# Expert outputs weighted on VectorE out of PSUM, and expert rows gathered one block earlier

## The chip, the cores and the metric

One core of a Trainium2 chip runs the whole program. It has five engines with queues of their own that run in order: TensorE (PE in the profile, its weight loads PEld), VectorE (DVE), ScalarE (ACT), GpSimd (POOL) and SyncE (SP), and 16 DMA engines that all queues share. The metric is the time of one execution in microseconds on the device; lower is better.

## What is computed

Two transformer-like blocks run one after the other on 512 tokens (plus 16 meta tokens in the first) of 1024 features. Only the last stage of the second block is touched, the mixture of experts:

```python
def block(args):                       # one padded group of rows of one expert
    tok, w, e = args
    y = swiglu(h[tok], w_gate[e], w_up[e], w_down[e])
    return y * w[:, None]
ys = lax.map(block, (row_tok..., row_w..., blk_e))
return jax.ops.segment_sum(ys.reshape(n_rows, d), row_tok, num_segments=n_tok)
...
x = x + g2 * moe_ffn(...)              # 64 experts, 6 of them for each token
return rms_norm(x, final_g)
```

Each token goes to 6 of 64 experts. An expert has a gate and an up matrix (1024 x 256 each) and a down matrix (256 x 1024). Its output rows are multiplied by the token's weight for this expert and by the vector `g2`, and added to the token's row. All of it is in fp32.

## The kernel before

Everything ahead of the experts (two mixers, the norm, the router, the shared expert) fills the first 2150 us of the span and is not touched. The router leaves index tables in SBUF: which token stands in which row of which block, and where its weight lies. `hn_d`, `w_d` and `moe_d` are DRAM tensors: the normed rows, the weights of (token, expert), and the sum that the experts add to.

The experts run as 31 units in a fixed `ORDER`. A unit is one expert with one or two blocks of rows: 128 and 128, 128 and 64, 128, 64, or 32. That makes 43 blocks: 24 of 128 rows, 7 of 64, 12 of 32. The first 37 blocks hold all those of 128 and 64 rows and 6 of 32; the last 6 are all of 32 rows. For one block the kernel does this:

- `Block.gather`: an indirect DMA on GpSimd's queue brings the rows of the block from `hn_d` into the tile `xg` (3 buffers).
- `Block.turn`: a second indirect DMA brings the 4-byte weights of the rows into `wg`; then `turned` transposes `xg` on TensorE into PSUM (`small`), and ScalarE and VectorE split it into a high and a low part (`exh`, `exl`).
- `Block.piece`: the next step of `expert`: the gate and up matmuls into PSUM (`proj`), SiLU on ScalarE and the product on VectorE (`ea`), two transposes, a split (`eah`, `eal`), and the down matmuls into the PSUM tile `big`, which the code calls `po`.
- `Block.add`, by `added`: ScalarE copies `po` times the weight into `ey` (2 buffers), GpSimd multiplies `ey` by `g2s`, and an indirect DMA on GpSimd's queue adds the rows of `ey` to `moe_d`. The last two blocks instead use two VectorE instructions that read PSUM and do both products at once. Below, that indirect DMA with the add is called the scatter.

The weights of an expert are three 1 MB tiles (`eraw`, 5 buffers, loaded by SyncE's queue), each split by ScalarE (`swh` or `ewh`) and VectorE (`swl` or `ewl`, 128x2048, the longest VectorE instructions of the stage).

The order on GpSimd's and SyncE's queue is that of the code, since both are under `manual_schedule`; on the other engines the scheduler keeps close to it. The loop runs over the blocks and works on three at a time. In turn `i` it finishes block `i-1`, turns block `i+1`, starts the matmuls of block `i`, gathers rows for block `i+2` and adds block `i-2`. A scatter waits for the one before it to have landed, since both add to `moe_d`. An instruction that writes `ey` waits until the scatter two blocks earlier has read and landed it.

```python
if i + 1 < len(blocks):
    blocks[i + 1].turn()
if b:
    if i:
        b.piece(4)
    if i and i + 2 < len(blocks):
        blocks[i + 2].gather()
...
if i > 1:
    blocks[i - 2].add()
```

Of the kernel before, what the change touches and what calls it, by code (L numbers as in the profile page):

```python
# [11 lines left out]
AF = mybir.ActivationFunctionType  # L12
# [1911 lines left out]

ORDER = [0, 19, 1, 20, 2, 15, 9, 12, 3, 21, 4, 22, 5, 16, 10, 13, 6, 23, 7, 24, 8, 17, 11, 14, 18, 25, 26, 27, 28, 29, 30]
STEPS = (0, 4, 10)
ROWS = SEQ + P


# [12 lines left out]
def moe(k, out):  # L1942
    nc, tc, io = k.nc, k.tc, k.io
    mult, add, sub = ALU.mult, ALU.add, ALU.subtract
    tt = nc.vector.tensor_tensor
    ts = nc.vector.tensor_scalar
    stt = nc.vector.scalar_tensor_tensor
    hn_d = k.dram.tile([ROWS, D], F32, name="hn_d")
    moe_d = k.dram.tile([ROWS, D], F32, name="moe_d")
    w_d = k.dram.tile([(SEQ + 1) * NE, 1], F32, name="w_d")  # L1950
# [6 lines left out]
    g2 = swp.tile([P, D], F32, name="g2s", bufs=1)  # L1957
# [139 lines left out]
    with ExitStack() as ctx:  # L2097
# [12 lines left out]
        def gather(bp, name, src, ix, bufs):  # L2110

            x = bp.tile([ix.shape[0], src.shape[1]], F32, name=name, bufs=bufs)
            nc.gpsimd.indirect_dma_start(out=x[:], out_offset=None, in_=src[:, :],
                                         in_offset=bass.IndirectOffsetOnAxis(ap=ix, axis=0))
            return x
# [26 lines left out]
                k.split(hi[:, j:j + nt], lo[:, j:j + nt], pt[:, :nt * n].rearrange("p (a b) -> p a b", a=nt))  # L2142
            return (lambda kt: (hi[:, kt], lo[:, kt])) if n == P else lambda kt: both[:, kt, :2 * n]

        def added(ix, wg, po, n, bp, last=False):

            y = bp.tile([n, D], F32, name="ey")
            if last:
                for hf in range(2):
                    sl = slice(hf * 512, hf * 512 + 512)  # L2150
                    stt(y[:, sl], po[0][:, hf], wg[:], g2[:n, sl], op0=mult, op1=mult)
            else:
                nc.scalar.activation(y[:].rearrange("p (a b) -> p a b", a=2), po[0], AF.Copy, scale=wg[:])  # L2153
                nc.gpsimd.tensor_tensor(y[:], y[:], g2[:n], op=mult)  # L2154
            nc.gpsimd.indirect_dma_start(out=moe_d[:, :], out_offset=bass.IndirectOffsetOnAxis(ap=ix, axis=0),  # L2155
                                         in_=y[:], in_offset=None, compute_op=add)

        with ExitStack() as c4:
# [55 lines left out]
            with tc.high_priority():  # L2214
# [7 lines left out]
                po = k.small()[:, :256].rearrange("p (a b) -> p a b", a=4)  # L2222
                for t in range(4):
                    for u in range(t + 1):
                        nc.tensor.matmul(po[:, t], lhsT=before if u == t else k.ones[:], rhs=mk[:, u], start=u == 0, stop=u == t)
            step(STEPS[0])

            with tc.high_priority():
# [16 lines left out]
                raws = [raw_of(es[0], i) for i in range(3)]  # L2245
            step(STEPS[1])

# [20 lines left out]
            with tc.high_priority():  # L2268
# [9 lines left out]
                sl = rp.tile([P, 4, TOPK], F32, name="sl")  # L2278
# [60 lines left out]
        ep = c3.enter_context(tc.tile_pool(reuse_waits="tile", name="mo_e", bufs=2))  # L2339
        bp = c3.enter_context(tc.tile_pool(reuse_waits="tile", name="mo_b", bufs=2))  # L2340
        wp = c3.enter_context(tc.tile_pool(reuse_waits="tile", name="mo_w", bufs=3, side="right"))
        class Block:
# [4 lines left out]
                self.ix, self.wx = idx[:self.n, col:col + 1], widx[:self.n, col:col + 1]  # L2347

            def gather(self):
                self.x = gather(bp, "xg", hn_d, self.ix, 3)  # L2350

            def turn(self):
                self.wg = gather(bp, "wg", w_d, self.wx, 4)
                self.po = []
                self.run = expert(turned(self.x, self.n, bp), self.n, self.unit.views, ep, self.po, AF.Silu)

# [2 lines left out]
                    next(self.run, None)  # L2359

            def add(self):
                added(self.ix, self.wg, self.po, self.n, ep, self in blocks[-2:])

        class Unit:
            def __init__(self, u, odd):
# [14 lines left out]
        blocks = [b for u in units for b in u.blocks]  # L2380
        ET = mybir.EngineType
        with tc.manual_schedule(engines={ET.Pool, ET.SP}):
            with tc.manual_schedule(engines={ET.PE, ET.Activation, ET.DVE}):
                blocks[0].gather()
                blocks[1].gather()
                nc.gpsimd.dma_start(w_d[:SEQ * NE].rearrange("(t p e) o -> p t (e o)", t=4, p=P), wd[:])
                blocks[2].gather()
                blocks[0].turn()
                units[0].weights(3 - len(units[0].w))
                units[1].weights(1)  # L2390
                blocks[0].piece(4)
            for i, b in enumerate(blocks + [None]):
                prev, ahead = blocks[i - 1] if i else None, []
                if i:
                    prev.piece()
                if i + 1 < len(blocks):
                    blocks[i + 1].turn()
                if b:
                    if i:
                        b.piece(4)  # L2400
                    if i and i + 2 < len(blocks):
                        blocks[i + 2].gather()
                    u = units.index(b.unit)
                    new = b is blocks[0] or b.unit is not prev.unit
                    if u + 1 < len(units):
                        ahead = [units[u + 1]] * (3 - len(b.unit.blocks))
                if i > 1:
                    blocks[i - 2].add()
                if b and new:
                    b.unit.weights(3 - len(b.unit.w))  # L2410
                if ahead:
                    u = ahead.pop()
                    u.weights(min(1, 3 - len(u.w)))
                if b:
                    b.piece()
                if i:
                    prev.piece(3)
                if ahead:
                    u = ahead.pop()
                    u.weights(min(1, 3 - len(u.w)))  # L2420
            blocks[-1].add()
        n = nc.values_load(nb_i[0:1, 0:1], min_val=0, max_val=(MB - NSTAT) // UNR,  # L2422
                           skip_runtime_bounds_check_because="at most MB columns")
        with tc.For_i(0, n, 1) as i:  # L2424
            ix = bp.tile([P, 2, UNR], I32, name="lix")
            be = bp.tile([1, UNR], I32, name="lbe")
            o = i * UNR + NSTAT
            nc.vector.tensor_copy(ix[:, 0], idx[:, bass.ds(o, UNR)])
            nc.vector.tensor_copy(ix[:, 1], widx[:, bass.ds(o, UNR)])
            nc.vector.tensor_copy(be[:], be_i[0:1, bass.ds(o, UNR)])  # L2430
            for u in range(UNR):
                e = nc.values_load(be[0:1, u:u + 1], engines=(mybir.EngineType.SP,), min_val=0, max_val=NE - 1,
                                   skip_runtime_bounds_check_because="six bits")
                x, wg = gather(bp, "xg", hn_d, ix[:, 0, u:u + 1], 3), gather(bp, "wg", w_d, ix[:, 1, u:u + 1], 4)
                ws, po = views([weights(e, j, u % 2) for j in range(3)]), []
                for _ in expert(turned(x, P, bp), P, ws, ep, po, AF.Silu):
                    pass
                added(ix[:, 0, u:u + 1], wg, po, P, ep)
# [9 lines left out]
        for t in range(4):  # L2448
            m, x = ms[t], fp.tile([P, D], F32, name="fx")
# [139 lines left out]
```

## Time and profile before

| | |
|---|---|
| median of 3 runs | 2648.27 us (2647.36 to 2651.03) |
| profiled execution, its own time | 2661.41 us |
| its span, from first to last instruction | 2659.4 us |
| mean granted TensorE clock | 0.934 |
| PE, DVE, ACT, POOL busy in the span | 87%, 70%, 50%, 41% |
| instructions | 41153 |

The busy shares are means over the whole program, and TensorE leads in them. The expert stage, from 2150 us on, is another picture: there the DMA engines are busy for four fifths of the time and GpSimd for three quarters, against a third each before it. What the change is worth must be read from that stage alone: from its windows, from who waited for whom in it, and from the order of time on GpSimd's queue.

### The profile page before, as it was taken

The page shows a single profiled execution, that of the slowest core. Times are in us where ns is not written, and L with a number is a line of the kernel's source. Part 1 is how long each engine was busy: PE and PEld are TensorE (multiplying, and loading weights), DVE is VectorE, ACT ScalarE, POOL GpSimd, SP SyncE. Part 2 cuts the span into 40 slices and gives each one's busy share as a digit, 9 for nine tenths or more (in the row PEclk, how much of TensorE's full clock was granted, in tenths as well). Part 3 has the DMA queues.
Part 4 walks back from the last instruction along what each step waited for, and adds up shares of the span by engine and source line. Part 5 has one row for each costly group of instructions (what it writes and reads, how often), then busy time and mean ns, then how long its engine had stood idle before and what let it go on. Part 6 is the DMA issues. An engine that isn't in the chain of part 4 may idle for free. (4 is left out here: it accounts for less than half of the span.)

```text
span 2659.4 us, 41153 instructions
## 1 busy us (share of the span) xinstructions
PE 2304.5 (87%) x15509; PEld 2016.5 (76%) x15509; DVE 1851.1 (70%) x3276; ACT 1334.1 (50%) x2302; POOL 1084.4 (41%) x694
## 2 busy tenths in 40 slices
PE   6989999999884899999889888988997988888884
PEld 5889999999874888888887887666777766666652
DVE  7788877878676477778878547766375576655575
ACT  5434433434421477777667535532345346555564
POOL 4234443333020454444444022433120048777786
PEclk9999999999996899999999998999798999988887
DMA  4222222222776422222111532233235178887885
GB/s 142 86 71 86 85 78 70 77 84 80 223 231 205 132 72 68 76 80 80 64 44 45 187 112 78 80 96 115 85 107 181 67 268 278 274 258 252 260 282 170
DMA packets 136367, 354.18 MB, mean 133 GB/s; under 512 B 26042, under 2 KB 51147, under 8 KB 124008
## 3 DMA queue, kind: packets, MB, share of 16 engines
q1 hardware_dynamic: 124120, 314.17, 35.4%
q0 software_dynamic: 10608, 32.14, 5.0%
q10 hardware_dynamic: 1440, 5.24, 0.6%
q8 instruction: 123, 2.02, 0.3%
q14 instruction: 76, 0.62, 0.1%
HBM read 301.54 MB, written 49.94 MB: 132 GB/s over the span
## 5 line engine op out<-in xcount | busy, mean ns | idle before, releaser
L180 POOL TENSOR_TENSOR wl<-wr,wh 128x1024 fp32r<-128x1024 f32 x159 | 409.6, 2578 | 629.1 <-ACT wh L179 523.1
L186 PE MATMUL proj<-yhi,wh 128*128 128x264 f32 (+2 forms) x1800 | 584.1, 325 | 11.8 <-ACT yhi L173 5.0
L187 PE MATMUL proj<-ylo,wh 128*128 128x264 f32 (+2 forms) x1800 | 577.8, 321 | 5.0 <-POOL ylo L180 3.2
L188 PE MATMUL proj<-yhi,wl 128*128 128x264 f32 (+2 forms) x1800 | 576.1, 320 | 0.0
L186 PEld LDWEIGHTS proj<-yhi,wh 128*128 128x128 f32 x1800 | 354.8, 197 | 33.2 <-ACT yhi L173 6.4
L187 PEld LDWEIGHTS proj<-ylo,wh 128*128 128x128 f32 x1800 | 354.5, 197 | 24.4 <-POOL ylo L180 4.1
L188 PEld LDWEIGHTS proj<-yhi,wl 128*128 128x128 f32 x1800 | 354.8, 197 | 20.5 <-issue 2.3
L179 ACT ACTIVATE wh<-wr 128x1024 fp32r<-128x1024 f32 x159 | 168.2, 1059 | 222.8 <-PE proj L187 166.9
L2155 POOL DMA_INDIRECT moe_d<-ey,idx x43 | 118.1, 2746 | 60.8 <-DMA moe_d<-ey,idx 30.6
L174 DVE TENSOR_TENSOR ewl<-eraw,ewh 128x2048 fp32r<-128x2048 f32 x45 | 111.9, 2489 | 32.7 <-ACT ewh L173 32.7
L174 DVE TENSOR_TENSOR swl<-eraw,swh 128x2048 fp32r<-128x2048 f32 x46 | 116.9, 2541 | 25.0 <-ACT swh L173 24.0
L186 PE MATMUL big<-oh,wh 128*128 128x256 f32 (+1 forms) x400 | 116.2, 295 | 17.7 <-ACT oh L173 7.6
L188 PE MATMUL big<-oh,wl 128*128 128x256 f32 (+1 forms) x400 | 115.9, 292 | 4.5 <-DVE wl L174 4.4
L187 PE MATMUL big<-ol,wh 128*128 128x256 f32 (+1 forms) x400 | 116.5, 294 | 0.1
L1176 ACT ACTIVATE ex<-big,mx 128x528 f32<-128x528 f32 x128 | 88.5, 696 | 55.0 <-DVE mx L1172 53.2
L2154 POOL TENSOR_TENSOR ey<-ey,g2s 128x1024 f32<-128x1024 f32 (+2 forms) x41 | 104.3, 2544 | 24.9 <-ACT ey L2153 24.0
L857 DVE SCALAR_TENSOR_TENSOR adw<-adw,ada_c 128x512 f32<-128x512 f32 x96 | 71.5, 756 | 46.5 <-DMA adw<-ada_w 45.8
L1172 DVE TENSOR_REDUCE mx<-big 128x1 f32<-128x528 f32 x128 | 84.9, 697 | 22.9 <-PE big L1171 22.6
L173 ACT ACTIVATE swh<-eraw 128x2048 fp32r<-128x2048 f32 x46 | 87.7, 1908 | 18.0 <-PE proj L188 14.8
L186 PEld LDWEIGHTS big<-oh,wh 128*128 128x128 f32 x400 | 78.1, 197 | 20.9 <-ACT oh L173 9.0
L2141 PE MATMUL small<-ident,xg 128*128 128x128 f32 (+2 forms) x344 | 45.4, 267 | 53.8 <-DMA xg<-hn_d,idx 52.2
L1056 ACT ACTIVATE sw<-proj 32x264 f32<-32x264 f32 (+1 forms) x192 | 86.5, 451 | 4.0 <-DVE qk L1053 1.2
(639 smaller groups left out, 6859.3 us busy)
## 6 DMA issues: line engine op xcount, KB each, us to landing
eraw<-ew SPq DMA_DIRECT2D x93, 1024.0 KB
wr<-hy_w SPq DMA_DIRECT2D x64, 512.0 KB
adw<-ada_w SPq DMA_DIRECT2D x96, 256.0 KB
wr<-mx_w SPq DMA_DIRECT2D x31, 512.0 KB
dm<-dmain SPq DMA_DIRECT2D x16, 512.0 KB
wr<-hy_wo SPq DMA_DIRECT2D x16, 512.0 KB
wr<-da_wz SPq DMA_DIRECT2D x16, 512.0 KB
wr<-da_wk SPq DMA_DIRECT2D x16, 512.0 KB
```

Of the source, the lines that this page charges most:

```text
L173: act = self.nc.scalar.activation(hi, src, AF.Copy)
L174: self.nc.vector.tensor_tensor(lo, src, hi.bitcast(F32), op=ALU.subtract)
L179: act = self.nc.scalar.activation(hi, src, AF.Copy)
L180: self.nc.gpsimd.tensor_tensor(lo, src, hi.bitcast(F32), op=ALU.subtract)
L186: mm(out, lhsT=a[0], rhs=b[0], start=start, stop=False)
L187: mm(out, lhsT=a[0], rhs=b[1], start=False, stop=False)
L188: mm(out, lhsT=a[1], rhs=b[0], start=False, stop=stop)
L1056: nc.scalar.activation(sw[a:a + 32, sl], ps[b:b + 32], AF.Copy, scale=sgn)
L1172: nc.vector.tensor_reduce(mx[:, m:m + 1], ps[:, :, :TH], axis=AX.XY, op=ALU.min)
L1176: nc.scalar.activation(e[:, :T].rearrange("p (a b) -> p a b", a=2), ps[:, :, :TH], AF.Exp, bias=mx[:, m:m + 1], scale=-1.0, accum_out=sm[: ...
L2154: nc.gpsimd.tensor_tensor(y[:], y[:], g2[:n], op=mult)
L2155: nc.gpsimd.indirect_dma_start(out=moe_d[:, :], out_offset=bass.IndirectOffsetOnAxis(ap=ix, axis=0), in_=y[:], in_offset=None, compute_op=add)
```

## The change

`added` loses its ScalarE and GpSimd instructions: every block is now weighted by two VectorE `scalar_tensor_tensor` instructions of 512 columns each, which read `po` in PSUM, the weight as a scalar of each row and `g2`, and write `ey`. The rows are gathered three blocks ahead (`AHEAD`) into 4 buffers instead of 3. The gather of the weights leaves `turn`: it is issued in the turn of the block itself, one turn later than before, and behind the gather of rows.

```diff
+AHEAD = 3
-        def added(ix, wg, po, n, bp, last=False):
+        def added(ix, wg, po, n, bp):
             y = bp.tile([n, D], F32, name="ey")
-            if last:
-                for hf in range(2):
-                    sl = slice(hf * 512, hf * 512 + 512)
-                    stt(y[:, sl], po[0][:, hf], wg[:], g2[:n, sl], op0=mult, op1=mult)
-            else:
-                nc.scalar.activation(y[:].rearrange("p (a b) -> p a b", a=2), po[0], AF.Copy, scale=wg[:])
-                nc.gpsimd.tensor_tensor(y[:], y[:], g2[:n], op=mult)
+            for hf in range(2):
+                sl = slice(hf * 512, hf * 512 + 512)
+                stt(y[:, sl], po[0][:, hf], wg[:], g2[:n, sl], op0=mult, op1=mult)
...
-                self.x = gather(bp, "xg", hn_d, self.ix, 3)
+                self.x = gather(bp, "xg", hn_d, self.ix, AHEAD + 1)
+            def weight(self):
+                self.wg = gather(bp, "wg", w_d, self.wx, 4)
             def turn(self):
-                self.wg = gather(bp, "wg", w_d, self.wx, 4)
...
-                blocks[2].gather()
+                for b in blocks[2:AHEAD]:
+                    b.gather()
...
-                    if i and i + 2 < len(blocks):
-                        blocks[i + 2].gather()
+                    if i + AHEAD < len(blocks):
+                        blocks[i + AHEAD].gather()
+                    b.weight()
```

On GpSimd's queue, from the turn of block 2 on (its gathers of weights and rows, its product and its scatter, for two blocks), there stood before:

```order
L2113 DMA wg<-w_d,widx 128x1
L2113 DMA xg<-hn_d,idx 128x1024
L2154 TENSOR_TENSOR ey<-ey,g2s 128x1024
L2155 DMA moe_d<-ey,idx 640x1024
L2113 DMA wg<-w_d,widx 128x1
L2113 DMA xg<-hn_d,idx 32x1024
L2154 TENSOR_TENSOR ey<-ey,g2s 128x1024
L2155 DMA moe_d<-ey,idx 640x1024
```

And in the changed kernel, from the same turn on, for three blocks:

```order
L2114 DMA xg<-hn_d,idx 32x1024
L2114 DMA wg<-w_d,widx 32x1
L2152 DMA moe_d<-ey,idx 640x1024
L2114 DMA xg<-hn_d,idx 128x1024
L2114 DMA wg<-w_d,widx 128x1
L2152 DMA moe_d<-ey,idx 640x1024
L2114 DMA xg<-hn_d,idx 128x1024
```

Each block now has three instructions there instead of four, the rows come first behind a scatter, and they are those of the block after the one that stood there before (the 32 rows are already gathered ahead of the first scatter).

On VectorE, where the stage's fourth block is turned (`exl`), before:

```order
L174 TENSOR_TENSOR eal<-small,eah 128x256
L174 TENSOR_TENSOR exl<-small,exh 128x512 x2
L174 TENSOR_TENSOR ewl<-eraw,ewh 128x2048
L1997 TENSOR_TENSOR elow<-proj,elow 32x512
L174 TENSOR_TENSOR ewl<-eraw,ewh 128x2048
```

And in the changed kernel:

```order
L174 TENSOR_TENSOR eal<-small,eah 128x256
L2151 SCALAR_TENSOR_TENSOR ey<-big,wg,g2s 128x512
L174 TENSOR_TENSOR exl<-small,exh 128x512
L2151 SCALAR_TENSOR_TENSOR ey<-big,wg,g2s 128x512
L174 TENSOR_TENSOR exl<-small,exh 128x512
L174 TENSOR_TENSOR ewl<-eraw,ewh 128x2048
L1998 TENSOR_TENSOR elow<-proj,elow 32x512
L2151 SCALAR_TENSOR_TENSOR ey<-big,wg,g2s 128x512 x2
L174 TENSOR_TENSOR ewl<-eraw,ewh 128x2048
```

The two products of a block stand between or ahead of the splits that TensorE's next block needs. ScalarE's and TensorE's work is otherwise the same, and SyncE's order does not change.

## Rows read from the trace of the kernel before

**Rows 1.** Windows: ahead of the experts and experts; busy PE, PEld, DVE, ACT, POOL, clock, DMA share, GB/s.

```profile
0.00:2150.00 2150.00, 1891.12 (x13601) 1719.11 (x13602) 1525.07 (x2976) 1042.93 (x1987) 712.75 (x515) 0.94 0.32 105
2150.00:2642.00 492.00, 413.42 (x1910) 297.37 (x1908) 320.93 (x297) 286.56 (x308) 365.51 (x171) 0.91 0.80 253
```

**Rows 2.** The same columns: first scatter to 38th, and from there to the end.

```profile
2190.00:2598.00 408.00, 349.49 (x1598) 255.08 (x1597) 263.80 (x227) 245.65 (x264) 318.20 (x148) 0.92 0.86 269
2598.00:2642.00 44.00, 27.65 (x123) 12.97 (x121) 29.24 (x25) 20.05 (x22) 31.90 (x13) 0.87 0.40 119
```

**Rows 3.** Waits, 2190 to 2598 us: engine, tile, line <- released by: us, times, longest.

```profile
PE small L2141 <- DMA xg<-hn_d,idx: 48.8, 11, 10.5
DVE eal L174 <- ACT eah L173: 45.7, 14, 6.2
...
POOL moe_d L2155 <- DMA moe_d<-ey,idx: 27.6, 9, 4.9
...
ACT ey L2153 <- DMA moe_d<-ey,idx: 19.3, 5, 5.5
...
POOL moe_d L2155 <- issue: 16.1, 5, 5.1
```

**Rows 4.** GpSimd in order of time: start us, us, instruction, [idle before it <- releaser].

```profile
2391.75 2.40 POOL L2154 TENSOR_TENSOR ey<-ey,g2s 128x1024 f32<-128x1024 f32 x1
2394.43 3.35 POOL L2155 DMA_INDIRECT moe_d<-ey,idx  x1 [0.28 <-POOL ey L2154]
...
2407.83 4.73 POOL L2155 DMA_INDIRECT moe_d<-ey,idx  x1 [5.06 <-issue]
...
2416.25 2.85 POOL L2113 DMA_INDIRECT xg<-hn_d,idx  x1 [0.30 <-issue]
...
2421.75 1.61 POOL L2155 DMA_INDIRECT moe_d<-ey,idx  x1 [0.28 <-POOL ey L2154]
```

**Rows 5.** TensorE in order of time: the longest of its waits for rows.

```profile
2427.21 1.09 PE L2141 MATMUL small<-ident,xg 128*128 128x128 f32 x4 [10.49 <-DMA xg<-hn_d,idx]
```

**Rows 6.** Waits of SyncE's queue, 2150 to 2640 us: its largest, for a free weight buffer.

```profile
SPq L2121 <- DVE ewl L174: 204.2, 31, 16.3
```

**Rows 7.** The tile ey, 2150 to 2640 us: count: duration ns min/median/max, first and last start.

```profile
L2153 ACT ACTIVATE ey<-big,wg x41: 1104/1115/1122, 2186.3 to 2619.9; 128x1024 f32<-128x1024 f32 x24, 32x1024 f32<-32x1024 f32 x10, 64x1024 f32<-64x1024 f32 x7
L2154 POOL TENSOR_TENSOR ey<-ey,g2s x41: 2354/2401/4297, 2187.5 to 2623.4; 128x1024 f32<-128x1024 f32 x24, 32x1024 f32<-32x1024 f32 x10, 64x1024 f32<-64x1024 f32 x7
```

**Rows 8.** Groups by shape, 2190 to 2598 us: count | busy us, mean ns | idle before.

```profile
L2155 POOL DMA_INDIRECT moe_d<-ey,idx x37 | 104.4, 2820 | 52.3 <-DMA moe_d<-ey,idx 27.6 <-issue 16.1 <-POOL ey L2154 8.6
L174 DVE TENSOR_TENSOR swl<-eraw,swh 128x2048 fp32r<-128x2048 f32 x39 | 99.8, 2560 | 19.5 <-ACT swh L173 18.5 <-issue 0.8
L174 DVE TENSOR_TENSOR ewl<-eraw,ewh 128x2048 fp32r<-128x2048 f32 x39 | 98.3, 2520 | 32.7 <-ACT ewh L173 32.7
```

**Rows 9.** VectorE in order of time: two weight splits beside GpSimd's rows above.

```profile
2391.60 4.71 DVE L174 TENSOR_TENSOR swl<-eraw,swh 128x2048 fp32r<-128x2048 f32 x1 [0.41 <-ACT swh L173]
...
2408.92 2.28 DVE L174 TENSOR_TENSOR swl<-eraw,swh 128x2048 fp32r<-128x2048 f32 x1
```

**Rows 10.** VectorE and GpSimd in order of time, among the last four blocks.

```profile
2628.26 0.74 DVE L2151 SCALAR_TENSOR_TENSOR ey<-big,wg,g2s 32x512 f32<-32x512 f32 x1 [0.28 <-PE big L188]
...
2627.98 1.36 POOL L2155 DMA_INDIRECT moe_d<-ey,idx  x1 [0.28 <-POOL ey L2154]
...
2638.03 1.32 POOL L2155 DMA_INDIRECT moe_d<-ey,idx  x1 [2.95 <-DMA moe_d<-ey,idx]
```

**Rows 11.** GpSimd: first and last pair of scatters where the second waited for the first.

```profile
2199.81 3.36 POOL L2155 DMA_INDIRECT moe_d<-ey,idx  x1 [0.28 <-POOL ey L2154]
...
2211.40 3.25 POOL L2155 DMA_INDIRECT moe_d<-ey,idx  x1 [2.40 <-DMA moe_d<-ey,idx]
...
2530.84 3.35 POOL L2155 DMA_INDIRECT moe_d<-ey,idx  x1 [0.28 <-POOL ey L2154]
...
2544.11 4.86 POOL L2155 DMA_INDIRECT moe_d<-ey,idx  x1 [4.94 <-DMA moe_d<-ey,idx]
```

More of the change, by code (lines that the diff above doesn't have):

```diff
@@ L2361, in add @@
             def add(self):
-                added(self.ix, self.wg, self.po, self.n, ep, self in blocks[-2:])
+                added(self.ix, self.wg, self.po, self.n, ep)
         class Unit:
@@ L2433, in moe @@
                                    skip_runtime_bounds_check_because="six bits")
-                x, wg = gather(bp, "xg", hn_d, ix[:, 0, u:u + 1], 3), gather(bp, "wg", w_d, ix[:, 1, u:u + 1], 4)
+                x, wg = gather(bp, "xg", hn_d, ix[:, 0, u:u + 1], AHEAD + 1), gather(bp, "wg", w_d, ix[:, 1, u:u + 1], 4)
                 ws, po = views([weights(e, j, u % 2) for j in range(3)]), []
```

## The prediction

> **What bounds the kernel now.** I read the windows first. TensorE leads in the whole span, but the change touches the experts alone, 492 of 2659 us. There the DMA engines are busy for 0.80 of the time against 0.32 before it, and GpSimd for 366 us of 492 [rows 1]. I split the stage where its character changes: 408 us between the first and the 38th scatter, in which 37 blocks are added (11.0 us each), and 44 us of small blocks at the end [rows 2].
>
> The waits of the long stretch come next. TensorE stands still for 48.8 us in 11 places, up to 10.5 us, for gathered rows. No other wait of TensorE is near that size: busy 349 plus 49 is 398 of 408, so outside these waits it is close to full. Its clock was granted at 0.92 there, a mix of both levels [rows 2, 3, 5].
>
> Why are the rows late? GpSimd's queue in order of time tells it. A scatter issued at 2394.43 had not landed when the next one's turn came; that one waited 5.06 us, then took 4.73 us to issue, and only behind it came the gather at 2416.25, whose rows TensorE got at 2427.21 [rows 4, 5]. Scatters are a chain, each waiting for the one before, and the gathers stand behind them in the same queue. In 14 of the 37 blocks GpSimd waited there (9 named as a DMA, 5 as issue, 43.7 us in all) [rows 3].
>
> Weights are not the bound. SyncE's queue waits 204 us for the split of one kind of tile alone to give back a buffer, so loads run ahead of their use [rows 6].
>
> **The rows' gathers, earlier.** A gather of block `i+3` now stands where that of `i+2` stood, and ahead of the weights' gather. That is one whole block of lead, 11.0 us, and the longest wait is 10.5, the mean 4.4 (48.8/11). The waits for rows should be gone, all 48.8 us of them, if nothing else is late. TensorE alone would then need 408 - 49 = 359 us.
>
> **What is late next: the chain of scatters.** The trace shows no landing of a single scatter, but where one waited for the one before, the distance between their starts is what the chain needs. There are 14 such pairs, the first 11.6 us (2199.81 to 2211.40), the last 13.3 (2530.84 to 2544.11), from 7.8 to 13.6, mean 11.35 [rows 11]. The earlier scatter of all of them has 128 rows. For 64 and 32 rows no pair exists in the stretch: from below stands the very end, with a nearly idle DMA, 1.32 + 2.95 = 4.3 us [rows 10], from above the 11.35 of 128 rows. I take 8, the middle. With 24 blocks of 128 rows and 13 smaller ones the chain needs 24 x 11.35 + 13 x 8 = 376 us; its ends are 272 + 56 = 328 and 272 + 148 = 420. The pairs that waited are the longer ones, so 376 leans high. It is later than TensorE's 359, so the chain is what is left: 408 - 376 = 32 us to gain, not 49.
>
> **DMA, pressed closer.** The same bytes in less time: 0.86 x 408 = 351 us of full DMA work, so at 383 us the share is 0.92. A scatter's packets then queue longer. How much, no row tells. From below it is nothing, or less than nothing, if scatters meet fewer splits; from above, 1.2 us each (44 us) takes more than the whole gain. I take 0.2 us for each of 37, 7 us, near the lower end, since 13.6 us, the longest pair, is already what a crowded DMA gives and the mean of 11.35 holds many such. The stretch comes to 383, which is 25 us less.
>
> **The weighting on VectorE.** Removed are 41 ScalarE copies of 1.12 us and 41 GpSimd products of 2.40 [rows 7]; 37 of them are 41 and 89 us in the stretch. GpSimd's part stood ahead of the scatter in its queue, yet where the chain waited anyway it was hidden. Added are two VectorE instructions for each block. The last blocks show their price, 0.74 us with 32 rows [rows 10]; the columns are the same 512 for 128 rows, and ScalarE's copy costs the same for 32 and 128 rows [rows 7], so 1.48 a block, 55 us in the stretch. Bounds: 1.12, were it as cheap as ScalarE's copy, and 2.40, GpSimd's price.
>
> Some of it comes back. A weight split costs 2.28 us alone and 4.71 when GpSimd's product of 2.40 starts in its first moments [rows 4, 9]. The 78 splits of the stretch took 99.8 + 98.3 = 198 us [rows 8]; at 2.28 they would take 178. So 20 us go with the products, and VectorE's load rises from 264 to 264 + 55 - 20 = 299 of 383 us, 0.78. It stays below the chain, and its added time is hidden while TensorE works on the next block's matmuls; were that cover gone, the price would be 55 - 20 = 35 us.
>
> The other direction counts too. The scatter at 2407.83 took 4.73 us to issue with a whole split of 2.28 inside it; the one at 2394.43 took 3.35 behind the end of the long split; the one at 2421.75 took 1.61 [rows 4, 9]. The new instruction seems not to do this: a scatter of 1.36 us overlapped one of 0.74, against 1.32 with nothing beside it [rows 10]. The Trainium skill, in "SBUF — State Buffer", section "Who interferes with whom", says that VectorE contends with GpSimd when both its inputs lie in SBUF and GpSimd reads SBUF, and not when at most one does. By that rule the new instruction, with one tensor in PSUM, leaves the scatters alone, as the 1.36 does; were it to hold them up, the whole 1.48 on 37 scatters would add 55 us and the sum would be 2679. The same section infers that an operation on two SBUF tensors does not delay the writing of descriptors; the 4.73 against 1.61 speaks against that, and the sum goes by the rows.
>
> **New waits.** Before, ScalarE waited for a free `ey`, 19.3 us in 5 places [rows 3]. Now VectorE waits for it, and behind it in its queue stand the second `exl` and a weight split. The wait ends when the scatter two blocks back has landed, so it is the same chain, felt on another engine; while the chain keeps its pace it costs nothing beyond the 383. The weights' gather is issued one turn later, but still ahead of the scatter whose landing the product waits for anyway, so it costs nothing; if the queue stood, its landing would add to that wait. The fourth gather ahead of the first scatter only fills GpSimd's idle time.
>
> **Start and end.** The first scatter starts 1.12 + 2.40 - 1.48 = 2 us earlier. In the last 44 us VectorE is busy 29 [rows 2], and four of the six blocks get 1.48 us more, 5.9 in all; I count half, 3 us (from -8, if the shorter way from PSUM to the scatter counts four times 2, to +6).
>
> **The sum.** -25 - 2 + 3 = -24 us. The profiled execution took 2661.4 us (span 2659.4), 13.1 over the median of the runs; it goes to 2637, and the runs from 2648.3 to 2624.
>
> **Rivals.**
> - *The chain is shorter than counted.* For it: the 14 pairs are the long ones, and scatters that start as soon as the one before lands stand beside the product out of PSUM rather than beside a split. Then TensorE is next: -49 - 2 + 3 = -48, and some unevenness between the engines takes a little, so about 2603. Against it: DMA's share would be 351/359 = 0.98.
> - *The gain is eaten by the DMA.* If each scatter needs 0.9 us more, the chain is 376 + 33 = 409 and the time stays at 2648. For it speaks the share of 0.92; against it, that the loads pause by themselves when buffers are full. That the rows still come late, so that the change does not do what it says, ends at the same place.
> - *Slower: VectorE's queue becomes the bound.* A block takes 11.0 us, of which VectorE works 7.1 and idles 3.9. The change adds 1.48 and gives 0.54 back (20/37), 35 us in all. If its idle time shrinks by less than that, the blocks get longer: half of TensorE's 48.8 lost again leaves 35 - 24 = +11, with the end +3, or 2662. For it: the products stand ahead of the `exl` that the next block needs. Against it: VectorE's largest idle time is behind `eah`, 45.7 us in 14 places [rows 3], much of which is the shadow of TensorE's waits and goes with them. The Trainium skill ("Perfetto Trace Analysis", "Optimizing Scalar/DVE Operations") advises to move work to ScalarE when VectorE is saturated, and this change goes the other way; by that rule this rival holds once VectorE is saturated. At 264 against ScalarE's 246 of 408 us it is not [rows 2].
>
> **How the numbers follow.** Chances: forecast 0.48 (alone 2612 to 2636), shorter chain 0.20, gain eaten 0.18, slower 0.14. A measurement of this kernel can tell 0.2%, 5.3 us, from no change. Faster by more: 0.48 + 0.20 and 0.05 of the third, 0.73. Within: 0.12 of the third. Slower: 0.14 and 0.01 of the third, 0.15. The range goes from 2598, below the second case by the 5 us that its unevenness may not cost, to 2656, which takes in the third and leaves out most of the fourth.
>
> **What would show it.** In the new profile TensorE's wait for `xg` should be under 10 us; GpSimd's wait for the scatter before should be in most blocks, in total above 43.7; splits should all be near 2.28; the new instruction should be near 0.74 for 128 rows; the stretch should take 375 to 392 us with a DMA share of 0.90 or more. The prediction is wrong if TensorE's waits for `exl`, `ea` or `eal` take the place of those for rows, or if pairs of scatters grow beyond 12.5 us in the mean.

## The result, and the profile after

The changed kernel takes 2609.6 us (median of four runs, 2599.6 to 2614.3) against 2649.7 of the kernel before: a ratio of 0.9829, 95% interval 0.9806 to 0.9853. The medians differ by 40 us, and the ratio on record stands for 45. Forecast were 24, or 2624 us, with a range that reaches down to 2598. The direction and most of the engine waits came out as forecast, the size was too small, and the cause turned out to be shared otherwise than the prediction had it.

The profiled execution after has a span of 2612.4 us, 47.0 less than the one before. First the windows, in the same columns as [rows 1, 2] (busy PE, PEld, DVE, ACT, POOL, clock, DMA share, GB/s): the long stretch from the first scatter to the 38th, and from there to the end.

```profile
2186.40:2556.20 369.80, 342.84 (x1610) 245.38 (x1609) 291.33 (x301) 209.95 (x227) 208.34 (x111) 0.96 0.94 295
2556.20:2595.00 38.80, 25.20 (x112) 11.47 (x112) 26.97 (x30) 16.39 (x20) 15.79 (x9) 0.89 0.44 136
```

The same 37 blocks take 369.8 us where they took 408 [rows 2], so 38 of the 47 us lie here; 4.7 more lie between the 38th and the 43rd scatter (39.6 to 34.9), and 3.8 ahead of the stage, where nothing was changed. VectorE has 28 us more to do and GpSimd 110 less. The DMA share rose from 0.86 to 0.94.

The waits of that stretch (engine, tile, line <- released by: us, times, longest), beside [rows 3]:

```profile
ACT eah L173 <- PE small L2008: 64.5, 22, 7.1
POOL moe_d L2152 <- DMA moe_d<-ey,idx: 49.4, 9, 6.8
DVE ey L2151 <- DMA moe_d<-ey,idx: 43.4, 11, 9.7
...
POOL moe_d L2152 <- issue: 41.5, 13, 7.3
...
POOL moe_d L2152 <- DVE ea L2004: 18.6, 7, 6.7
...
PE small L2008 <- DVE ea L2004: 13.5, 6, 3.9
...
PE big L188 <- DVE eal L174: 10.5, 3, 4.8
```

TensorE's 48.8 us for rows are gone: from 2150 to 2600 us one such wait is left.

```profile
PE small L2142 <- DMA xg<-hn_d,idx: 2.6, 1, 2.6
```

A part came back as TensorE's waits for `ea` and `eal`, 24 us together. In the kernel before they had been 8 (2190 to 2598 us):

```profile
PE big L188 <- DVE eal L174: 5.0, 5, 1.4
PE small L2007 <- DVE ea L2003: 3.1, 2, 1.8
```

Two engines now wait for a scatter to land: GpSimd before it issues the next one, and VectorE before it may write a new `ey`. The groups by shape (count | busy us, mean ns | idle before, its releasers) and the tile `ey` answer to [rows 7, 8]:

```profile
L174 DVE TENSOR_TENSOR swl<-eraw,swh 128x2048 fp32r<-128x2048 f32 x39 | 89.2, 2286 | 4.8 <-ACT swh L173 4.7
L174 DVE TENSOR_TENSOR ewl<-eraw,ewh 128x2048 fp32r<-128x2048 f32 x39 | 89.0, 2283 | 8.9 <-ACT ewh L173 8.8
L2152 POOL DMA_INDIRECT moe_d<-ey,idx x37 | 87.2, 2356 | 149.0 <-DMA moe_d<-ey,idx 49.4 <-issue 41.5 <-DVE ea L2004 18.6
```

```profile
L2151 DVE SCALAR_TENSOR_TENSOR ey<-big,wg,g2s x86: 728/741/753, 2184.1 to 2587.6; 128x512 f32<-128x512 f32 x48, 32x512 f32<-32x512 f32 x24, 64x512 f32<-64x512 f32 x14
L2152 POOL DMA_INDIRECT moe_d<-ey,idx x43: 1313/1606/7732, 2186.4 to 2591.1; - x43
```

The splits are all at 2.28 us, the new instruction takes 0.741 us for any number of rows, and GpSimd sits idle 149 us in front of its 37 scatters where it sat 52.3 [rows 8]. It is a queue that waits for one thing: the scatter before.

### The chain, scatter by scatter

The prediction said that the trace shows no landing of a single scatter. It does: a scatter has 16 completion signals among the trace's semaphore events (for a few scatters fewer are recorded, two of the first 37 in the trace of before), and the last of them can be taken for its landing. With that the stretch divides without rest into 37 times (start to landing) and 37 gaps (landing to the start of the next). The shortest gaps are some 0.78 us, 29 us for 37; below they are called the floor. These sums are worked out from the trace of each kernel; "transfer" is from the end of the issue to the landing.

| kernel | stretch | start to landing | gaps | mean issue | mean transfer |
|---|---|---|---|---|---|
| before | 408.3 | 336.9 | 71.4 | 2.82 | 6.29 |
| after | 369.8 | 334.5 | 35.4 | 2.36 | 6.68 |
| after, a second profile | 358.6 | 324.8 | 33.7 | 2.15 | 6.63 |
| gathers only | 391.5 | 326.3 | 65.2 | 2.41 | 6.41 |
| weighting only | 375.1 | 319.4 | 55.7 | 2.24 | 6.39 |
| after, half splits | 348.6 | 318.6 | 29.9 | 1.83 | 6.78 |
| after, half the weight bytes | 334.3 | 286.0 | 48.2 | 2.42 | 5.31 |
| before, half splits | 369.8 | 297.6 | 72.2 | 2.14 | 5.90 |

So the change left the chain's links as long as they were (issue 37 x 0.46 = 17 us shorter, transfer 37 x 0.39 = 14 us longer) and closed the gaps between them: from 42.6 us over the floor to 6.6. Before, 21 of the 37 scatters started at the floor, 0.76 to 0.81 us after the landing of the one before; the other 16 started 1.7 to 8.1 us after it, each straight behind its product on GpSimd. After, 32 of 37 start at the floor: the chain sets the pace. Two profiles of the same changed kernel differ by 11 us in the stretch, so smaller differences between single profiles are not read below; the ratios, made from several runs, are.

### The profile page after: what moved, and what is told of

Its sections match the earlier page's. It is cut to its first block, busy times and chain, and to the rows that moved or that the text cites. A ratio compares the mean times of both kernels' runs of the same rounds, so it can differ in the third digit from the quotient of the medians.

```text
span 2612.4 us, 41156 instructions
## 1 busy us (share of the span) xinstructions
PE 2293.4 (88%) x15509; PEld 2005.3 (77%) x15509; DVE 1876.8 (72%) x3358; ACT 1293.0 (49%) x2261; POOL 954.6 (37%) x653
## 5 line engine op out<-in xcount | busy, mean ns | idle before, releaser
L2152 POOL DMA_INDIRECT moe_d<-ey,idx x43 | 99.4, 2312 | 170.7 <-DMA moe_d<-ey,idx 52.3
L174 DVE TENSOR_TENSOR swl<-eraw,swh 128x2048 fp32r<-128x2048 f32 x46 | 105.1, 2286 | 8.2 <-ACT swh L173 8.0
L174 DVE TENSOR_TENSOR ewl<-eraw,ewh 128x2048 fp32r<-128x2048 f32 x45 | 102.7, 2283 | 8.9 <-ACT ewh L173 8.8
L173 ACT ACTIVATE ewh<-eraw 128x2048 fp32r<-128x2048 f32 x45 | 85.7, 1909 | 33.8 <-PE big L188 23.6
L2151 DVE SCALAR_TENSOR_TENSOR ey<-big,wg,g2s 128x512 f32<-128x512 f32 (+2 forms) x86 | 61.5, 739 | 56.2 <-DMA moe_d<-ey,idx 43.4
```

The costliest lines, as they stand in the source:

```text
L173: act = self.nc.scalar.activation(hi, src, AF.Copy)
L174: self.nc.vector.tensor_tensor(lo, src, hi.bitcast(F32), op=ALU.subtract)
```

## Experiments

Ratios are to the kernel before on the same chip, with 95% intervals. In the order of the questions.

### Which half of the change brings the gain?

The earlier gathers with the old weighting:

```
-            for hf in range(2):
-                ... stt(y[:, sl], po[0][:, hf], wg[:], g2[:n, sl], ...)
+            nc.scalar.activation(y[:]..., po[0], AF.Copy, scale=wg[:])
+            nc.gpsimd.tensor_tensor(y[:], y[:], g2[:n], op=mult)
```

> Only the new order of the gathers (rows three blocks ahead, in front of the weights' gather); the outputs are weighted as before, by ScalarE and GpSimd. Theory CHAIN (the waits for rows went because the gathers are a block earlier, and the chain of scatters is the bound now): GpSimd's product of 2.4 us fits into the time in which the queue waits for the scatter before, so most of the gain stays: 25 to 38 us under the kernel before, no wait of TensorE for rows over 10 us in all. Theory RELIEF (GpSimd's queue was simply too full, and taking 2.4 us a block out of it brought the gain): within 10 us of the kernel before.

Measured: 0.9959 (0.9936 to 0.9982), 2646.9 us: by the ratio 11 us, at the edge of RELIEF's 10, where the prediction's theory CHAIN wanted 25 to 38. TensorE waits 2.7 us for rows, so this half does what it says. Its stretch (the windows' columns) and two of its waits:

```profile
2196.60:2588.10 391.50, 343.38 (x1605) 246.22 (x1603) 286.18 (x228) 246.58 (x266) 320.55 (x148) 0.95 0.90 282
```

```profile
ACT ey L2154 <- DMA moe_d<-ey,idx: 40.8, 8, 7.7
...
PE small L2008 <- DVE ea L2004: 33.8, 15, 7.2
```

The rows arrive, and TensorE waits elsewhere: ScalarE holds its queue for a free `ey` (40.8 us where it was 19.3 [rows 3]), and `ea` and `eal` come late behind it. GpSimd is busy for 320.6 of 391.5 us, and each DMA of its queue has some 0.3 us ahead of it in which it isn't counted as busy.

The weighting on VectorE with the old gathers (the kernel before, with the new `added`):

> Only the weighting on VectorE; the gathers stand as before, two blocks ahead and behind the weights' gathers. CHAIN: the gathers still stand behind a scatter that waits for the one before, so TensorE still waits 25 to 45 us for rows, and the gain is 5 to 15 us. RELIEF: 30 to 40 us under the kernel before, waits for rows under 10 us.

Measured: 0.9909 (0.9882 to 0.9936), 2631.0 us: 24 us, twice as much, though TensorE still stands for rows. Its stretch, and TensorE's wait for rows from 2150 to 2600 us:

```profile
2193.20:2568.30 375.10, 340.24 (x1601) 246.74 (x1600) 292.30 (x301) 211.82 (x228) 194.49 (x112) 0.95 0.93 293
```

```profile
PE small L2141 <- DMA xg<-hn_d,idx: 26.0, 10, 6.0
```

Half of the wait for rows is gone without any earlier gather, since a gather that stands behind a shorter queue is early by itself. So the larger part of the gain comes with GpSimd's product leaving the scatters' queue, as RELIEF had said; the prediction had called that product hidden. Neither theory had the numbers: 24 us lie between CHAIN's 5 to 15 and RELIEF's 30 to 40, and the 26.0 us of waits in CHAIN's 25 to 45. By the table about half of the shorter stretch are closed gaps (71.4 to 55.7 us) and half are shorter links (336.9 to 319.4). By the ratios the halves of the change are worth 11 and 24 us, both together 42 to 45; that their sum falls short by 7 to 10 is about what the intervals leave open, and that the halves help each other is not excluded.

### Is the chain of scatters what is left?

Every other of the first 37 blocks is added to a second, zeroed tensor, which is read and added at the end. Each sum then has half the chain.

```
+    moe_e = k.dram.tile([ROWS, D], F32, name="moe_e")
...
-                added(self.ix, self.wg, self.po, self.n, ep)
+                added(self.ix, self.wg, self.po, self.n, ep, moe_e if self.odd_sum else moe_d)
+            b.odd_sum = i % 2 == 1 and i < 37
...
+            tt(m[:], m[:], m2[t // 2][:, t % 2 * D:t % 2 * D + D], op=add)
```

> The changed kernel with the chain cut in two: of the first 37 blocks every other one is added to a second, zeroed sum in DRAM, which is read and added at the end (2.6 MB more written ahead of the experts, 2 MB more read at the end). CHAIN: the stretch from first to 38th scatter shrinks from 370 us to 348 to 358, the end costs 5 us more, so 2592 to 2604 against 2609.6 of the changed kernel. Theory DMA (the 16 DMA engines, at a share of 0.94 in that stretch, are the bound by now): the stretch stays at 365 to 372 with the same share, and the time is 2610 to 2617.

Measured: 0.9787 (0.9725 to 0.9848), 2594.9 us; the interval is wide and reaches up to the changed kernel's 0.983 to 0.984, so the stretch must decide. It went from 369.8 (358.6 in the second profile) to 336.5 us, more than CHAIN had asked, and some 6 us went back at the end, where the second sum is read.

```profile
2193.10:2529.60 336.50, 330.42 (x1598) 239.25 (x1597) 289.59 (x300) 208.62 (x226) 209.58 (x111) 0.99 1.00 323
```

```profile
POOL moe_d L2153 <- DVE ey L2152: 70.6, 16, 12.2
...
POOL moe_e L2153 <- DVE ey L2152: 37.5, 12, 7.8
```

Scatters now wait for their product and no longer for each other. TensorE is busy for 330.4 of 336.5 us and the DMA for all of it. VectorE has the same load as before this edit (290 us), and TensorE's wait for `ea` falls from 13.5 to 3.5 us, so VectorE had not been the bound. The chain was the bound of the changed kernel's stretch, and it was worth some 22 to 33 us there. With half splits beside it (below) the gain over the changed kernel is clear of the intervals too.

### Is VectorE's added time hidden?

Each product is computed twice.

```
-            for hf in range(2):
+            for hf in (0, 1, 0, 1):
```

> The changed kernel with each block's two weighting instructions on VectorE issued twice (the second pair writes the same values): 1.48 us more VectorE work a block, 64 us in all, 55 in the stretch of 37 blocks. CHAIN: VectorE waits for a free output tile anyway, so most of it is hidden: 0 to 12 us over the changed kernel, 2610 to 2622. Theory VECTORE (VectorE's queue is the bound now, 291 of 370 us busy): 35 to 60 us over it, 2645 to 2670.

Measured: 0.9933 (0.9912 to 0.9955), 2641.0 us, between the two theories. 86 more instructions of 0.74 us are 64 us; against the changed kernel's 0.984 they cost 0.0093 of 2650, about 25 us. VectorE is busy 336.7 of 380.0 us of the stretch:

```profile
2198.90:2578.90 380.00, 341.09 (x1597) 242.92 (x1596) 336.74 (x374) 212.53 (x227) 178.67 (x111) 0.97 0.90 285
```

The stretch grew by 10 us (21 against the second profile) and the last five blocks by 8. So VectorE isn't the bound, but its time is not free either: the second dose of 1.48 us a block costs about two fifths of itself. How much of the first dose is paid was not separated.

### Is it the tile `ey` or the queue?

The earlier gathers left ScalarE waiting for a free `ey`. Three of them in place of two, with the old weighting and with the new:

```
-            y = bp.tile([n, D], F32, name="ey")
+            y = bp.tile([n, D], F32, name="ey", bufs=3)
```

> The kernel with only the new order of the gathers (weighting by ScalarE and GpSimd), with three output tiles instead of two. There the wait for rows was gone, but ScalarE waited 40.8 us for a free output tile, and the stretch from first to 38th scatter took 391.5 us against 369.8 in the changed kernel. Theory TILE (the longer way through ScalarE and GpSimd keeps the two output tiles busy, so the chain of scatters has gaps): with a third tile the stretch falls to 368 to 378. Theory QUEUE (GpSimd's queue itself is full: 321 of 391 us busy and about 44 us between instructions): it stays at 385 to 394, although ScalarE's wait for a tile falls under 10 us.

> The changed kernel with three output tiles instead of two. VectorE waited 43.4 us for a free one in the stretch. Theory CHAIN (scatters follow each other without a gap, so a tile that comes free earlier moves nothing): VectorE's wait falls, GpSimd's wait for the scatter before rises, the stretch stays at 365 to 372 us and the time within 8 us of the changed kernel (0.983 of the kernel before). Theory TILE (VectorE's wait for the tile is what stops TensorE): the stretch falls to 345 to 358.

Measured: 0.9972 (0.9950 to 0.9993) with the old weighting, where two tiles gave 0.9959; 0.9874 (0.9822 to 0.9926) with the new, where two gave 0.984. Neither gains; the stretches were 397.1 and 376.9 us, a little above what QUEUE (385 to 394) and CHAIN (365 to 372) gave. The wait changed its name, with the old weighting and with the new:

```profile
ACT ey L2154 <- DMA wg<-w_d,widx: 35.2, 8, 8.4
```

```profile
DVE ey L2151 <- DMA wg<-w_d,widx: 29.2, 6, 7.5
```

The weights stand in GpSimd's queue behind a scatter that waits for the one before. A free buffer lets no one pass a queue that is in order; TILE came true in neither. TensorE even waits for rows again, 9.1 and 14.5 us from 2150 to 2600 us. With the old weighting the gaps did shrink (65.2 to 45.0 us), as TILE had them, but the links grew by more (326.3 to 352.1); why they grew is not shown.

### What makes a link of the chain long?

Half of the weights' bytes are not loaded:

```
-            nc.sync.dma_start(raw[:], io["ew"]...)
-            split(w[0][:], w[1][:], raw[:])
+            nc.sync.dma_start(raw[:, :D], io["ew"]...[:, :D])
+            two = lambda x: x[:].rearrange("p (a b) -> p a b", a=2)
+            split(two(w[0]), two(w[1]), raw[:, None, :D].to_broadcast([P, 2, D]))
```

> The changed kernel with only the first half of each expert weight tile loaded (512 KB instead of 1 MB; the splits read that half twice, so every engine's work is the same and the experts compute with wrong weights). It measures how far the load on the DMA engines lengthens a scatter. CHAIN: a scatter's way from start to landing falls from 8.5 us in the mean to 6.5 or less, gaps open in the chain, TensorE sets the pace, and the stretch takes 335 to 350 us. If instead the scatters' own latency, free of the load, sets the chain, they stay above 8 us and the stretch above 360.

Measured: 0.9759 (0.9715 to 0.9803), 2595.1 us; the stretch 334.3 us, at a DMA share of 0.80 and 205 GB/s. The transfer of a scatter fell from 6.68 to 5.31 us (37 x 1.37 = 51 us), start to landing to 7.73. The 6.5 that were expected of the latter at most were not reached: the issue stayed at 2.42 us (2.36), with half the bytes beside it. Part of the 51 came back as gaps (48 us where there were 35): the blocks were then late instead, with TensorE busy for 328.9 of the 334.3 us.

The weights' split in two halves of 1024 columns, on the changed kernel:

```
+        def halves(hi, lo, src):
+            nc.scalar.activation(hi, src, AF.Copy)
+            for h in range(2):
+                sl = slice(h * D, h * D + D)
+                tt(lo[:, sl], src[:, sl], hi[:, sl].bitcast(F32), op=sub)
...
-        def weights(e, i, odd, split=k.split):
+        def weights(e, i, odd, split=halves):
```

> The changed kernel with VectorE's weight splits of 2048 columns issued as two of 1024. If a split holds GpSimd up only while it runs, GpSimd gets in between the halves: the scatters' issue falls from 2.36 us to under 2.0 in the mean, its longest from 7.7 to under 4, and the stretch from 369.8 to 355 to 364, less what 78 x 0.15 us more on VectorE take back. If GpSimd does not get in between, issue and stretch stay as they are or grow by up to 8 us.

Measured: 0.9785 (0.9741 to 0.9828), 2600.4 us; stretch 348.6, below what either theory gave. Nothing was taken from VectorE's work: two halves take 2 x 1.216 us for 2.28. The interval overlaps that of the changed kernel a little. But the scatters' issue fell from 2.36 to 1.83 us in the mean, 20 us over 37. The scatters (min/median/max ns) and the halves:

```profile
L2158 POOL DMA_INDIRECT moe_d<-ey,idx x43: 1314/1602/3967, 2182.8 to 2568.6; - x43
```

```profile
L2129 DVE TENSOR_TENSOR swl<-eraw,swh 128x1024 fp32r<-128x1024 f32 x79 | 94.7, 1216 | 8.5 <-ACT swh L2126 8.5
```

The longest issue went from 7.73 to 3.97 us. What the 7.73 had been shows in GpSimd's and in VectorE's order of time of the changed kernel (start us, us, instruction, [idle before it <- releaser]):

```profile
2263.36 1.47 POOL L2152 DMA_INDIRECT moe_d<-ey,idx  x1 [6.74 <-DVE ea L2004]
...
2271.69 7.73 POOL L2152 DMA_INDIRECT moe_d<-ey,idx  x1 [3.02 <-DVE ea L2004]
...
2288.15 1.48 POOL L2152 DMA_INDIRECT moe_d<-ey,idx  x1 [6.19 <-DMA moe_d<-ey,idx]
```

```profile
2272.54 2.27 DVE L174 TENSOR_TENSOR ewl<-eraw,ewh 128x2048 fp32r<-128x2048 f32 x1
...
2275.67 2.27 DVE L174 TENSOR_TENSOR swl<-eraw,swh 128x2048 fp32r<-128x2048 f32 x1
...
2287.48 1.41 DVE L2151 SCALAR_TENSOR_TENSOR ey<-big,wg,g2s 128x512 f32<-128x512 f32 x2 [8.61 <-DMA moe_d<-ey,idx]
```

Two whole splits lie inside the issue of 7.73 us; the two around it took 1.47 and 1.48. The order of time of all 43 scatters says the same: in the kernels before and after, the issue of every scatter that met no split took 1.31 to 1.63 us, also of those that ran beside the new instruction for up to 1.3 us. And the last row shows the price: VectorE itself then waits 8.61 us for the landing that its own splits have delayed.

The same halves on the kernel before:

> The kernel before, with VectorE's weight splits of 2048 columns issued as two of 1024 and nothing else. In the changed kernel this cut the scatters' issue from 2.36 to 1.83 us and the stretch from 370 to 349. Theory QUEUE (before, the chain had gaps because GpSimd's queue was full: 318 of 408 us busy, a third of that with waiting behind splits): the stretch falls from 408 to 372 to 392 and the waits for rows from 48.8 to under 30 us, with no gather moved. Theory LEAD (only an earlier gather helps): the stretch stays above 400 and the waits for rows above 40.

Measured: 0.9902 (0.9872 to 0.9932), 2628.8 us: as much as the whole weighting on VectorE brings, with no queue's order and no gather changed.

```profile
2192.80:2562.60 369.80, 338.06 (x1600) 244.77 (x1598) 288.77 (x302) 242.78 (x265) 285.66 (x148) 0.97 0.93 295
```

```profile
PE small L2147 <- DMA xg<-hn_d,idx: 20.4, 11, 6.3
```

GpSimd's busy time falls from 318 [rows 2] to 286 us for the same 148 instructions, and TensorE's wait for rows from 48.8 to 20.4 us, without a gather being earlier in the queue. LEAD is refuted, and QUEUE's numbers came (the stretch 2 us better than its 372 to 392), but not by its mechanism: the gaps in the chain did not close (71.4 us before, 72.2 now). All 38 us come out of the links, 25 from the issue (2.82 to 2.14) and 14 from the transfer (6.29 to 5.90, although the DMA share rose from 0.86 to 0.93; why is open). The late rows were thus relieved by shorter links as well as by a shorter queue.

### What bounds it next, and the order of the two gathers

Two sums and half splits together:

> The changed kernel with both: two sums and half splits. Alone they took the stretch from 369.8 to 336.6 (DMA share 1.00) and 348.6 (0.98). Theory DMA (once the chain gives way, the 16 DMA engines and TensorE, granted 0.99 of its clock there, are the bound): no shorter than with two sums, 332 to 340, time 0.977 to 0.981 of the kernel before. Theory CHAIN (scatters still set the pace): 315 to 328, 0.970 to 0.975.

Measured: 0.9775 (0.9750 to 0.9801), 2597.9 us (four runs, 2595.2 to 2601.2), beside 2613.6 (2609.0 to 2616.9) of the changed kernel in the same series: 15.6 us faster than the changed kernel, and 59 than the kernel before. From the two sums alone (0.9787) it can't be told apart.

```profile
2194.90:2524.10 329.20, 325.72 (x1589) 237.52 (x1587) 290.46 (x372) 204.75 (x222) 158.66 (x112) 1.00 1.00 326
```

The DMA's share is 1.00, TensorE is busy for 325.7 of 329.2 us: two bounds at once, and the stretch just under what the DMA theory gave.

The weights' gather ahead of the rows' gather:

```
+                    b.weight()
                     if i + AHEAD < len(blocks):
                         blocks[i + AHEAD].gather()
-                    b.weight()
```

> The changed kernel with the two gathers of a turn swapped back: weights first, rows behind them, still three blocks ahead. If the lead of a block is what counts and their order nothing: stretch 365 to 375 and no wait for rows over 5 us in all. If the place ahead of the weights' gather counts: rows waited for 10 us or more and the stretch 376 to 385.

Measured: 0.9871 (0.9840 to 0.9903), TensorE's wait for rows 2.2 us, stretch 367.6. The interval overlaps that of the changed kernel (0.9840, 0.9815 to 0.9865), so no difference is shown, though up to some 0.7% is not excluded; with either order the block more of lead brings the rows.

The changed kernel again:

> The changed kernel once more, on the chip of the three others. CHAIN: stretch 365 to 375 us, scatters waiting for the one before in nearly all blocks, time 0.980 to 0.986 of the kernel before.

Measured: 0.9840 (0.9815 to 0.9865), as at first; the stretch was 358.5 us, below the 365 to 375 that were expected of it, with the DMA at 0.97. The mean of the time is stable, the stretch of one profile is not.

```profile
2194.00:2552.50 358.50, 338.26 (x1611) 242.66 (x1609) 291.84 (x301) 210.80 (x229) 202.80 (x111) 0.98 0.97 306
```

## Why the prediction was right, and where it wasn't

**Right.** *Rows' waits*: forecast under 10 us, 2.6 measured. *What is late next*: the chain of scatters; 32 of 37 start at the floor, and two sums show it. The trace can tell more than the 14 waits that the prediction counted: by the landings the chain was at the floor in 21 of the 37 blocks before. *VectorE*: splits at 2.28, the new instruction at 0.741 for 128 rows, load 291 us (forecast 299) or 0.79 of the stretch. *DMA*: 0.94, forecast 0.90 or more. The rival "VectorE becomes the bound" fell, but not without a trace: it wanted half of TensorE's 48.8 us lost again, and the waits for `ea` and `eal` rose from 8 to 24 us, a third of it; with two sums the wait for `ea` fell to 3.5. The Trainium skill ("Perfetto Trace Analysis", "Optimizing Scalar/DVE Operations") says that moving some work from a saturated VectorE to ScalarE may make sense. At 0.79 it wasn't saturated here, and even a doubled dose cost only 25 of 64 us. The rival "eaten by the DMA" fell too, though its cause was real: the transfer got longer by 0.4 us.

**Terms of the sum that were mis-sized.**

| term | forecast | measured |
|---|---|---|
| chain without more load | 376 | 336.9 + 28.8 = 366 |
| DMA pressed closer, 37 x | 0.2 = +7 | 0.39 = +14 |
| issue of 37 scatters | 0 | -17 |
| gaps over the floor | 0 | +7 |
| stretch | 383 | 370 (358.5 in the second profile) |
| start | -2 | 0 |
| from the 38th scatter on | +3 | -5 |

*The chain, 376.* It came from the 14 pairs that waited, of 11.35 us in the mean, and the text said that they lean high. They did: the 24 scatters of 128 rows of the kernel before take 9.61 us from start to landing, and 0.78 to the next, 10.4 in all, 23 us less for the 24. The 13 smaller ones were put too low, 8 for 8.97, 13 us the other way, so that 10 are left.

*The issue, 0.* This is the largest miss. The working had the rows for it, 4.73, 3.35 and 1.61 [rows 4], but put it only into the lower bound ("less than nothing, if scatters meet fewer splits"). They did meet fewer: summed over the 37 issues, splits ran beside them for 64 us before and for 37 after. That a split of 2.28 covers less of GpSimd's time than one of 4.71 is one reason that can be argued, but not the whole: with the earlier gathers alone, which keep the products, the sum was 50 us and the mean issue 2.41. The Trainium skill, "SBUF — State Buffer", section "Who interferes with whom", says that a VectorE instruction with two inputs in SBUF contends with a GpSimd instruction that reads SBUF, and that one with at most one such input, outside the two-port modes, doesn't contend. The runs agree for both: a split of 2.28 us took 4.71 beside GpSimd's product [rows 9], and the new instruction, with one input in PSUM, left the scatters' issue at a median of 1.6 us. The section's inference that a `tensor_tensor` on two SBUF inputs doesn't delay the writing of descriptors is not borne out: 7.73 us around two splits, 1.47 without.

*The start, -2.* The first scatter comes 30.55 us after the first gather, 30.61 before: ScalarE's and GpSimd's 3.5 us against VectorE's 1.48 had not been on the path there.

*The end, +3.* VectorE's 1.48 us were counted, and GpSimd's 2.4 only in the lower bound (-8). GpSimd in order of time shows why the sign was wrong, first before, then after:

```profile
2598.44 3.13 POOL L2155 DMA_INDIRECT moe_d<-ey,idx  x1 [0.28 <-POOL ey L2154]
2601.88 2.82 POOL L2113 DMA_INDIRECT wg<-w_d,widx  x1 [0.30 <-issue]
2605.00 2.32 POOL L2113 DMA_INDIRECT xg<-hn_d,idx  x1 [0.30 <-issue]
2607.35 4.25 POOL L2154 TENSOR_TENSOR ey<-ey,g2s 32x1024 f32<-32x1024 f32 x1
2611.88 3.46 POOL L2155 DMA_INDIRECT moe_d<-ey,idx  x1 [0.28 <-POOL ey L2154]
```

```profile
2556.20 1.37 POOL L2152 DMA_INDIRECT moe_d<-ey,idx  x1 [2.17 <-DVE swl L174]
2557.88 0.89 POOL L2114 DMA_INDIRECT wg<-w_d,widx  x1 [0.30 <-issue]
2564.71 3.32 POOL L2152 DMA_INDIRECT moe_d<-ey,idx  x1 [5.94 <-DVE elow L1998]
```

Before, GpSimd has no idle time from one scatter to the next beyond its own 0.3 us: 13.4 us of its own instructions, a product of 4.25 among them. After, 8.5 us with 5.9 of waiting.

**The step that was wrong.** "GpSimd's part stood ahead of the scatter in its queue, yet where the chain waited anyway it was hidden." In 21 blocks it was, the 14 that were counted and 7 more. In the other 16 the scatter before had landed, the next was issued straight behind its product, and there the product was on the path; these 16 hold the 42 us of gaps over the floor. The sum gives the product's going no term of its own. The trace of before showed GpSimd busy for 318 us [rows 2] and, ahead of its DMAs, pauses of some 0.3 us [rows 4], 31 us in all without the waits: 349 of 408 us together; all that is left of the stretch are 43.7 us of waits at scatters [rows 3] and one more wait, of the product for ScalarE's copy (2190 to 2598 us):

```profile
POOL ey L2154 <- ACT ey L2153: 14.3, 6, 5.4
```

The prediction took the waits for rows as the thing removed and the chain as the limit of the gain; the runs show the late rows as one symptom of a queue in which product, gathers and scatters followed each other, and the earlier gathers alone gave a quarter of the 42 to 45 us. The sum came out as near as it did because both halves end at the same chain; that is luck as far as the cause goes. And it is not very near: 2609.6 lies below the forecast's own band (2612 to 2636) and closer to the rival "shorter chain" (2603). That rival was right that the chain was shorter than counted, and wrong that TensorE would then be next: the changed kernel still ran at the chain.

**The floor of TensorE, 359**, was not one either: the two sums took 336.5 us. TensorE's busy time for these blocks fell from 349.5 us at a granted clock of 0.92 [rows 2] to 342.8 at 0.96, 330.4 at 0.99 and 325.7 at 1.00, of which 1.00 is the upper of its two levels, 2.4 GHz, throughout. So with the waits some of the busy time goes too, and that rival was priced too high by it.

**Left open.** What the first 1.48 us a block on VectorE cost; what shortened the issue where the products stayed; why half splits alone shortened the transfer; why two profiles of one kernel differ by 11 us in the stretch.

## What to carry to other kernels

An engine that issues DMAs in order is a resource like the others: count its busy time plus the 0.3 us ahead of each DMA, and where that comes near the span, take work out of that queue before moving its gathers forward. A chain of accumulating scatters into one tensor is broken by a second tensor, and its links are shortened by what stands beside them (a long VectorE instruction on two SBUF inputs in two halves) as well as by less DMA load. Before a wait is taken for the cause, ask what the instruction that ends it stood behind.

## What the runs showed of the hardware

- A scatter's issue on GpSimd takes 1.3 to 1.6 us alone or beside a VectorE instruction with one input in PSUM, and up to 7.73 beside two VectorE splits of 2.28 us on SBUF operands. Halving these instructions, with no work taken away, brought the kernel before to 0.9902, and the changed one from 0.984 to 0.9785 (intervals that overlap by a little).
- A scatter of 128 rows of 4 KB took 9.6 us from start to landing in the mean in the kernel before (DMA share 0.86), 10.1 and 9.6 in two profiles of the changed kernel (0.94 and 0.97), 8.6 with half the weight bytes (0.80), and 8.8 in the kernel before with half splits (0.93). So the DMA share alone does not set it. The next scatter started some 0.78 us after its landing at the earliest.
- TensorE's granted clock rose from 0.92 to 1.00 as its waits in this stretch went, and nearly the same records of matmuls (1598 and 1589) took 24 us less.
